# One weight ring of five buffers, and PSUM banks of its own for the first block's second half, in a diffusion layer with PEER experts

## The chip, the cores and the metric

The kernel runs on one core of a Trainium2 chip. The metric is the device time of one execution in microseconds (us). A core has a matrix engine (PE, TensorE), VectorE (DVE), ScalarE (ACT), GpSimd (POOL) and SyncE (SP). Each takes its instructions in order. Matmuls write into PSUM, which has eight banks of 512 float32 in each of 128 partitions; the other data lie in SBUF. Transfers are issued by SP, ACT and POOL and run on 16 DMA engines.

## What is computed

One layer over 1024 latent tokens of width 1024, with 256 context tokens that give keys and values alone. All is float32. Cut to what matters:

```python
hx = modulate(rmsnorm(xs, norm1_g), sh1, sc1)
q, k, v, u, ga, gc = split(hx @ w_in)                  # w_in: 1024 x 5632
y_att  = attend(rope(norm(q)), rope(norm(k)) + k_ctx, v + v_ctx) @ w_attn_o
a, b   = split(u); g = a * sigmoid(b)
g      = depthwise_conv(g, width 31)                   # over the tokens, per channel
y_conv = silu(layernorm(g + conv_b)) @ w_conv_o
xs = xs + g1 * ((sigmoid(ga) * y_att + sigmoid(gc) * y_conv) @ w_out)
h  = modulate(rmsnorm(xs, norm2_g), sh2, sc2)
# PEER: 8 heads, two halves of 128 keys, the 16 best of each, the 16 best of their sums
s = h @ peer_wq, scored against peer_keys; eid, w = the 128 experts of a token and their weights
act = gelu(peer_u[eid] . h)                            # 128 rows of 1024 for each token
xs  = xs + g2 * sum((w * act) * peer_v[eid])
out = rmsnorm(xs, final_norm_g)
```

## The kernel before

**Blocks.** The tokens go in four blocks of 256 (two tiles of 128). For each block `phase1` makes four streams. `convolution` projects w_in's columns for the convolution into pb and pa and runs 31 taps for each of eight channel groups on DVE (`tap`, into z and odd). `attention` projects q (pq of 128 columns), norms and turns it, and does eight heads for each tile (pS the scores, pr the softmax, pt its transposes, po the product). `rest` is the second half of a block: the two gated products (`gated`, pg and py), between them the norm over channels (`channel_norm`, pmu and pvar, for which all taps must be done), the product with w_out (po of 256 columns, into dT), `second_norm` (transposes pt of dT, of xn and of h2T), and eight times `scores` (pq of 256 columns, then s2). `choosing` picks the 16 best on DVE. When two heads of a tile are chosen, their experts can be gathered.

**The experts.** `dots` gathers one row of peer_u for each of 128 tokens by an indirect DMA of POOL (tile u, 512 KB), and one DVE operation multiplies and sums it: one dot for each of 128 experts of a tile, 1024 in all. Three buffers hold u (`U_ROWS`) while the blocks run; when they are over, four more come from the space of the blocks (`U_MORE`). For five tiles (`GATHERED`) `sums_by_choice` gathers peer_v likewise (tile vv; three buffers, later nine) and PE adds it up in y by matmuls of 32 columns. For the other three (`DENSE`, tiles 1, 2 and 4) the dense stage at the end (`dense`) builds matrices of weights in four quarters (DVE makes B and A, PE pc, ACT C), and multiplies them with the whole of peer_v, loaded as vd: acc, 32 loads for each quarter. `finish_token_tile` does the last norm and the store.

**What sets the order.** Instructions are not issued as the streams write them. Each is recorded with a cost (`Paced`), and `Pace` keeps a model of each engine's time and emits next what can start first; nearly equal starts go by the rank of the stream. On DVE while the blocks run that rank is `RANK = "vumbahc"`: v rows, then dots (u), then a block's second half (m), the builds (b), attention (a), choosing (h), and the convolution with its taps (c) last. The names of a tile that is overwritten enter the model (`evicts`), so the number of buffers of a pool changes the order on all engines. All of it is at line 262 in the profile; groups are told apart by their tiles.

**Buffers that matter here.** `wload` loads a weight tile of 512 KB into the ring w; it has four buffers (`WEIGHTS`), and the transposed tokens hT of the start use the same ring. `bank` gives one of two PSUM banks (pool psm) to all that the blocks compute except pS: convolution, attention, and second half alike. `pair` halves one of them. The pool psy has one buffer of two banks: at the start pk (keys and values, one bank) takes it, later y. `rsqrt` has two scratch tiles of its own in the pool att for the norm over channels.

Of the kernel before, what the change touches and what calls it, by code (L numbers as in the profile page):

```python
# [8 lines left out]
F32 = mybir.dt.float32  # L9
# [3 lines left out]
AF = mybir.ActivationFunctionType  # L13
# [26 lines left out]
KEPT = 4  # L40
WEIGHTS, SLOTS, U_ROWS, V_ROWS, U_MORE, V_MORE = 4, 4, 3, 3, 4, 6

# [251 lines left out]
def layer_kernel(ctx: ExitStack, tc: tile.TileContext, a, out):  # L294
# [12 lines left out]
    exq = pool(ctx, "exq", 2)  # L307
    psy = pool(ctx, "psy", 1, space=PSUM)
    ps = pool(ctx, "ps", 1, space=PSUM)
# [18 lines left out]
    def pair(name):  # L328

        t = bank(name)  # L330
        return t[:, 0:256], t[:, 256:512]
# [4 lines left out]
    def rsqrt(y, v, n):  # L336

        home, tag = (small, n) if n < P else (att, "")
        t = home.tile([P, n], F32, name="rs_t", tag=f"rs_t{tag}", bufs=1)
        b = home.tile([P, n], F32, name="rs_b", tag=f"rs_b{tag}", bufs=1)  # L340
        V.tensor_scalar(t.bitcast(I32), v.bitcast(I32), 1, None, op0=OP.logical_shift_right)
        V.tensor_scalar(y.bitcast(I32), t.bitcast(I32), -1.0, float(0x5F3759DF), op0=OP.mult, op1=OP.add)
        for _ in range(3):
            V.tensor_tensor(out=b, in0=y, in1=y, op=OP.mult)
            V.scalar_tensor_tensor(out=b, in0=b, scalar=-0.5, in1=v, op0=OP.mult, op1=OP.mult)
            V.scalar_tensor_tensor(out=y, in0=b, scalar=1.5, in1=y, op0=OP.add, op1=OP.mult)
# [266 lines left out]
    def phase1(b, t0, Tb):  # L613
# [6 lines left out]
        mine = blocks[b] = {}  # L620

        def convolution():
            while b and "gated" not in blocks[b - 1]:
# [111 lines left out]
        def gated(g0, wo, src, first, mg):  # L735

            for j in range(KC):
                yield "PE"
                wg, w2 = wload(a["w_in"], g0 + j * P), wload(a[wo], j * P)
                pg, py = pair("pg")  # L740
                mm8(pg[:, :Tb], wg, lambda kc: mine["hT"][:, kc, :Tb])
                mm8(py[:, :Tb], w2, lambda kc: src[:, kc, :])
                tb = att.tile([P, Tb], F32, name="tg", tag="gt")
                S.activation(tb, pg[:, :Tb], AF.Tanh, scale=0.5)
                if first:
                    V.scalar_tensor_tensor(out=mg[:, j, :], in0=tb, scalar=1.0, in1=py[:, :Tb], op0=OP.add, op1=OP.mult)
                else:
                    V.scalar_tensor_tensor(out=tb, in0=tb, scalar=1.0, in1=py[:, :Tb], op0=OP.add, op1=OP.mult)
                    V.scalar_tensor_tensor(out=mg[:, j, :], in0=tb, scalar=0.5, in1=mg[:, j, :], op0=OP.mult, op1=OP.add)

        def channel_norm(z):

            yield "PE"
            pmu = bank("pmu")
            for j in range(KC):
# [4 lines left out]
            for j0 in range(0, KC, 4):  # L760
                yield "DVE"
                sq = [att.tile([P, Tb], F32, name="zsq", tag="zsq", bufs=4) for _ in range(4)]
                for j in range(4):
                    V.tensor_tensor(out=z[:, j0 + j, :], in0=z[:, j0 + j, :], in1=mu, op=OP.subtract)
                    S.activation(sq[j], z[:, j0 + j, :], AF.Square)
                pvar = bank("pvar")
                for j in range(4):
# [19 lines left out]
        def second_norm(i, dT, h2T):  # L787
# [5 lines left out]
            for half in range(2):  # L793
                pt = bank("pt")
                for q in range(4):
# [9 lines left out]
            for half in range(2):  # L805
                pt = bank("pt")
                for q in range(4):
# [6 lines left out]
            for half in range(2):  # L814
                pt = bank("pt")
                for q in range(4):
                    PE.transpose(pt[:, q * P:(q + 1) * P], h2T[:, half * 4 + q, ts], ident)
                S.activation(xn[:, half * 512:(half + 1) * 512], pt, AF.Copy)
            S.dma_start(h2_d[row, :], xn)

        def scores(q, h2T):
# [3 lines left out]
            q2 = att.tile([P, 2, Tb], F32, name="q2", bufs=1)  # L825
            pqs = pair("pq")
            for b in range(2):
# [4 lines left out]
            for i in range(nt):  # L832
                yield "PE"
                s2 = bank("s2")
                for b in range(2):
# [5 lines left out]
        def rest():  # L841
# [10 lines left out]
            for j in range(KC):  # L852
                yield "PE"
                w = wload(a["w_out"], j * P)
                po = bank("po")
                mm8(po[:, :Tb], w, lambda kc: mg[:, kc, :])
# [180 lines left out]
    def finish_token_tile(ti, y):  # L1037
# [5 lines left out]
        Q.dma_start(fin, a["final_norm_g"].to_broadcast([P, D]))  # L1043
        V.tensor_tensor(out=y, in0=y, in1=ga2, op=OP.mult)
        V.tensor_tensor(out=fo, in0=fo, in1=y, op=OP.add)
        ss = small.tile([P, 1], F32, name="ss", tag="ss1")
        S.activation(y, fo, AF.Square, accum_out=ss)
        r_ = rstd_of(ss, 1, D)
        V.scalar_tensor_tensor(out=fo, in0=fo, scalar=r_, in1=fin, op0=OP.mult, op1=OP.mult)
        S.dma_start(out[row, :], fo)  # L1050

    def dense():
# [67 lines left out]
        def products():  # L1120
# [4 lines left out]
            for n, ti in enumerate(DENSE):  # L1125
                finish_token_tile(ti, ysum[:, n, :])

        return building(), products()

    def sums_by_choice(ti, eiT, cT):  # L1130

        y = psy.tile([P, D], F32, name="y")
        for r in range(32):
# [9 lines left out]
            while j0 < 4:  # L1143
# [9 lines left out]
                for half in range(2):  # L1153
                    hs = slice(half * 512, (half + 1) * 512)
                    for j, vv in group[-1:] + group[:-1]:
                        PE.matmul(y[32 * j:32 * j + 32, hs], lhsT=Z[:, j, 32 * rr:32 * rr + 32], rhs=vv[:, hs],
                                  start=(r == 0), stop=(r == 31))
# [111 lines left out]
```

## Time and profile before

| | |
|---|---|
| median of 3 runs | 4075.68 us (4071.9 to 4087.45) |
| profiled execution: time | 4076.87 us |
| profiled execution: span of the instructions | 4075.1 us |
| PE busy | 3193.5 us (78%) |
| DVE busy | 2637.7 us (65%) |
| POOL busy | 1859.3 us (46%) |
| ACT busy | 759.9 us (19%) |
| moved by DMA | 1189.76 MB, mean 292 GB/s |

Busy time of PE is that of its matmul records, which overlap a little; a float32 matmul stands in the trace as two records, a transpose and a bf16 matmul as one. "PEclk" is the share of the 2.4 GHz that the chip grants the matrix engine, 1.00 or 0.50 at any moment. "DMA share" is the mean busy share of the 16 DMA engines. A row "A <- B: us, times" in the waits says how long A's engine stood idle until B released it.

### The profile page before, as it was taken

What the parts mean: (1) busy time and instruction counts of PE and PEld (TensorE: products, weight loads), DVE (VectorE), ACT (ScalarE), POOL (GpSimd) and SP (SyncE); (2) the same over time, 40 slices, a digit from 0 to 9 for tenths busy, and PEclk for the clock granted to TensorE, in tenths of its full rate; (3) what the DMA queues carried; (4) which work ended last, traced back from release to release, by engine and by line L of the source; (5) the groups of instructions that cost most, each with busy time, mean ns of one, the idle gap of its engine ahead of it and who ended that gap; (6) DMA issues with size and microseconds to landing.
All of it is one profiled execution on the core that took longest, in us unless ns stands there. A gap on an engine that the chain in (4) does not pass through costs nothing. (4 is left out here: it accounts for less than half of the span.)

```text
span 4075.1 us, 49507 instructions
## 1 busy us (share of the span) xinstructions
PE 3193.5 (78%) x17804; PEld 2009.4 (49%) x17804; DVE 2637.7 (65%) x7114; ACT 759.9 (19%) x1439; POOL 1859.3 (46%) x1672
## 2 busy tenths in 40 slices
PE   5898997779878889978656875468978866885994
PEld 2576885568655558745445742133443324332331
DVE  2493158887768896778888569685784458356102
ACT  3335113331012331023321020120020002001000
POOL 0000000443545553445444445686787768676550
PEclk9999998889889899989877987569979887997997
DMA  8530553779999889998779998899999999999993
GB/s 291 162 101 7 150 151 104 239 232 314 317 320 310 296 303 331 347 333 297 255 230 284 316 347 278 297 345 389 385 362 398 406 379 362 402 406 370 352 374 136
DMA packets 649558, 1189.76 MB, mean 292 GB/s; under 512 B 36825, under 2 KB 387393, under 8 KB 649312
## 3 DMA queue, kind: packets, MB, share of 16 engines
q0 software_dynamic: 239616, 872.52, 58.8%
q1 hardware_dynamic: 394736, 294.88, 23.6%
q10 hardware_dynamic: 14960, 19.19, 1.3%
q8 instruction: 140, 2.29, 0.2%
q14 instruction: 106, 0.87, 0.1%
HBM read 1168.62 MB, written 17.83 MB: 291 GB/s over the span
## 5 line engine op out<-in xcount | busy, mean ns | idle before, releaser
L262 POOL DMA_INDIRECT u<-in_peer_u,ei x1024 | 1117.2, 1091 | 1735.5 <-DVE tx L262 721.6
L262 DVE CUSTOM_DVE_ANT_0 u<-u,h 128x1024 f32<-128x1024 f32 x1024 | 1244.5, 1223 | 671.9 <-DMA u<-in_peer_u,ei 662.2
L262 POOL DMA_INDIRECT vv<-in_peer_v,eiT x640 | 739.1, 1155 | 392.1 <-PE y L262 192.5
L262 PE MATMUL y<-vv,Z 128*32 128x512 f32 x2560 | 509.2, 722 | 247.1 <-DMA vv<-in_peer_v,eiT 246.9
L262 PE MATMUL acc<-vd,C 128*128 128x512 f32 x1536 | 697.9, 607 | 0.0
L262 PEld LDWEIGHTS acc<-vd,C 128*128 128x128 f32 x1536 | 288.8, 194 | 398.3 <-issue 394.7
L262 PEld LDWEIGHTS y<-vv,Z 128*32 128x32 f32 x2560 | 95.2, 122 | 523.0 <-issue 280.0
L262 PE MATMUL pc<-A,B 128*128 128x32 bf16 x4608 | 179.1, 192 | 149.6 <-DVE A L262 131.5
L262 PEld LDWEIGHTS <-B 128*128 128x128 bf16 x4608 | 167.3, 118 | 215.2 <-DVE A L262 116.3
L262 PE MATMUL pq<-h2T,w 128*128 128x256 f32 x1024 | 248.0, 397 | 14.2 <-ACT q L262 7.3
L262 PE MATMUL pg<-hTb,w 128*128 128x256 f32 x1024 | 238.1, 385 | 6.7 <-DVE tg L262 3.6
L262 PEld LDWEIGHTS pq<-h2T,w 128*128 128x128 f32 x1024 | 198.4, 198 | 74.7 <-issue 23.9
L262 DVE SCALAR_TENSOR_TENSOR z<-g,dw,z 128x256 f32<-128x256 f32 x480 | 230.4, 480 | 0.0
L262 PE MATMUL pS<-kT,qT 128*128 128x512 f32 (+1 forms) x384 | 179.6, 585 | 54.8 <-ACT pr L262 54.8
L262 PE MATMUL pb<-hTb,w 128*128 128x256 f32 (+2 forms) x896 | 211.3, 389 | 13.0 <-DMA w<-in_w_in 9.2
L262 ACT ACTIVATE C<-pc 128x512 f32<-128x512 f32 x96 | 104.6, 1096 | 622.3 <-PE pc L262 373.9
L262 PEld LDWEIGHTS pg<-hTb,w 128*128 128x128 f32 x1024 | 195.8, 193 | 40.5 <-DVE tg L262 5.5
L262 DVE SCALAR_TENSOR_TENSOR odd<-g,dw,odd 128x256 f32<-128x256 f32 x448 | 215.1, 480 | 0.0
L262 PEld LDWEIGHTS pb<-hTb,w 128*128 128x128 f32 x896 | 171.8, 196 | 46.0 <-issue 19.6
L262 PEld LDWEIGHTS po<-pT,vS 128*128 128x128 f32 x1280 | 165.4, 204 | 37.0 <-issue 17.3
L262 PE MATMUL po<-pT,vS 128*128 128x128 f32 x1280 | 173.5, 290 | 6.6 <-ACT pT L262 6.0
L262 DVE TENSOR_TENSOR B<-io__15984,i12T 128x2048 bf16<-128x2048 bf16 x96 | 117.4, 1223 | 63.2 <-PE pc L262 57.3
(209 smaller groups left out, 3547.7 us busy)
## 6 DMA issues: line engine op xcount, KB each, us to landing
w<-in_w_in SPq DMA_DIRECT2D x160, 512.0 KB, 6.3
vd<-in_peer_v SPq DMA_DIRECT2D x128, 512.0 KB, 8.1
w<-in_peer_wq SPq DMA_DIRECT2D x64, 512.0 KB, 7.5
wm<-in_w_mod SPq DMA_DIRECT2D x48, 512.0 KB, 6.4
w<-in_w_attn_o SPq DMA_DIRECT2D x32, 512.0 KB, 6.1
w<-in_w_conv_o SPq DMA_DIRECT2D x32, 512.0 KB, 5.4
w<-in_w_out SPq DMA_DIRECT2D x32, 512.0 KB, 9.9
u<-in_peer_u,ei POOLq DMA_INDIRECT x1024, 7.0
```

Source lines behind the costliest of these rows:

```text
L262: go = lambda: f(*args, **kw)
```

## The change

Four things, all in how buffers are given out; the work is the same but for the last norm.

1. `WEIGHTS` is 5 instead of 4. The space comes in part from `rsqrt`, whose two scratch tiles of 256 columns are now taken from the ring zsq (four buffers, otherwise for the squares of the norm over channels).
2. The pool psy has two buffers of one bank instead of one of two banks. So pk of the start has two banks in turn, and y is two tiles of 512 columns, each a half.
3. In block 0 `gated`, `channel_norm`, `second_norm`, `scores` and the product with w_out take their PSUM tiles from psy (`bank2`), not from the pair that convolution and attention use. In the other blocks they stay where they were.
4. `finish_token_tile` works on the two halves one after the other, with two partial sums of squares and one addition more.

```diff
-WEIGHTS, SLOTS, U_ROWS, V_ROWS, U_MORE, V_MORE = 4, 4, 3, 3, 4, 6
+WEIGHTS, SLOTS, U_ROWS, V_ROWS, U_MORE, V_MORE = 5, 4, 3, 3, 4, 6
...
-    psy = pool(ctx, "psy", 1, space=PSUM)
+    psy = pool(ctx, "psy", 2, space=PSUM)
...
     def pair(name):
 
-        t = bank(name)
+        return halved(bank(name))
+
+    def halved(t):
         return t[:, 0:256], t[:, 256:512]
...
-        home, tag = (small, n) if n < P else (att, "")
-        t = home.tile([P, n], F32, name="rs_t", tag=f"rs_t{tag}", bufs=1)
-        b = home.tile([P, n], F32, name="rs_b", tag=f"rs_b{tag}", bufs=1)
+        t, b = ((small.tile([P, n], F32, name=m, tag=f"{m}{n}", bufs=1) if n < P else
+                 att.tile([P, n], F32, name=m, tag="zsq", bufs=4)) for m in ("rs_t", "rs_b"))
...
+        def bank2(name):
+
+            return bank(name) if b else psy.tile([P, 512], F32, name=name, tag="y")
...
-                pg, py = pair("pg")
+                pg, py = halved(bank2("pg"))
...
-            pmu = bank("pmu")
+            pmu = bank2("pmu")
...
-                pt = bank("pt")
+                pt = bank2("pt")
...
-            pqs = pair("pq")
+            pqs = halved(bank2("pq"))
...
-                po = bank("po")
+                po = bank2("po")
...
-        V.tensor_tensor(out=y, in0=y, in1=ga2, op=OP.mult)
-        V.tensor_tensor(out=fo, in0=fo, in1=y, op=OP.add)
-        ss = small.tile([P, 1], F32, name="ss", tag="ss1")
-        S.activation(y, fo, AF.Square, accum_out=ss)
-        r_ = rstd_of(ss, 1, D)
+        ss = small.tile([P, 2], F32, name="ss", tag="ss2")
+        for h in range(2):
+            hs = slice(h * 512, (h + 1) * 512)
+            V.tensor_tensor(out=y[h], in0=y[h], in1=ga2[:, hs], op=OP.mult)
+            V.tensor_tensor(out=fo[:, hs], in0=fo[:, hs], in1=y[h], op=OP.add)
+            S.activation(y[h], fo[:, hs], AF.Square, accum_out=ss[:, h:h + 1])
+        V.tensor_tensor(out=ss[:, 0:1], in0=ss[:, 0:1], in1=ss[:, 1:2], op=OP.add)
+        r_ = rstd_of(ss[:, 0:1], 1, D)
...
-        y = psy.tile([P, D], F32, name="y")
+        y = [psy.tile([P, 512], F32, name="y") for _ in range(2)]
```

The order changes on every engine, as the model behind it sees other buffers. Two places follow. A row is an instruction, its tiles, the size of its output, and how many of it stand in a row.

First place, PE, block 0's second norm (transposes pt of dT, xn and h2T), before. The matmuls pb and pq<-w,hTb are block 1's projections for convolution and attention.

```order
L262 MATMUL pt<-ident,dT 128x128 x4
L262 MATMUL pb<-hTb,w 128x256 x10
L262 MATMUL pt<-ident,dT 128x128 x4
L262 MATMUL pt<-ident,xn 128x128 x8
L262 MATMUL pt<-ident,h2T 128x128 x8
L262 MATMUL pt<-ident,dT 128x128 x8
L262 MATMUL pt<-ident,xn 128x128 x8
L262 MATMUL pt<-ident,h2T 128x128 x8
```

The same place now.

```order
L262 MATMUL pt<-ident,dT 128x128 x8
L262 MATMUL pb<-hTb,w 128x256 x15
L262 MATMUL pt<-ident,xn 128x128 x8
L262 MATMUL pq<-w,hTb 128x128 x8
L262 MATMUL pb<-hTb,w 128x256 x3
L262 MATMUL pt<-ident,h2T 128x128 x8
L262 MATMUL pq<-w,hTb 128x128 x3
L262 MATMUL pt<-ident,dT 128x128 x8
L262 MATMUL pq<-w,hTb 128x128 x5
L262 MATMUL pb<-hTb,w 128x256 x14
L262 MATMUL pq<-w,hTb 128x128 x8
L262 MATMUL pb<-hTb,w 128x256 x2
```

Block 1's projections stand between the steps of the second norm now, where before only one group of them did; the second token tile's xn transposes follow these rows.

Second place, PE, the end of block 1's gated products and the close of block 0's choice (pt of eid and e, whose results the v gathers and the dense stage use; pt of act is the end of the first tile's dots), before.

```order
L262 MATMUL pg<-z,w 128x256 x8
L262 MATMUL pt<-ident,eid 128x128
L262 MATMUL pt<-ident,e_1320 128x128 x2
L262 MATMUL pb<-hTb,w 128x256 x38
L262 MATMUL pq<-w,hTb 128x128 x8
L262 MATMUL pb<-hTb,w 128x256 x2
L262 MATMUL pq<-w,hTb 128x128 x4
L262 MATMUL pt<-ident,act 128x128
```

The same transposes of eid, e and act now.

```order
L262 MATMUL po<-pT,vS 128x128 x10
L262 MATMUL pt<-ident,eid 128x128
L262 MATMUL pt<-ident,e_1320 128x128 x2
L262 MATMUL pmu<-z,ones_d 128x256 x8
L262 MATMUL pt<-ident,act 128x128
L262 MATMUL pg<-hTb,w 128x256 x2
L262 MATMUL pvar<-zsq,ones_d 128x256
```

Before, block 1's norm over channels and all 256 of its gated matmuls (pg) stood ahead of the close of block 0's choice. Now that close and the end of the first tile's dots come first, and the gated matmuls behind them.

## Rows read from the trace of the kernel before

**Rows 1.** The page: span; DMA busy in tenths, 40 equal slices.

```profile
span 4075.1 us, 49507 instructions
DMA  8530553779999889998779998899999999999993
```

**Rows 2.** Tile u, 720 to 973 us: count, duration, first and last start.

```profile
L262 DVE CUSTOM_DVE_ANT_0 u<-u,h x96: 1203/1224/1279, 720.3 to 966.7; 128x1024 f32<-128x1024 f32 x96
```

**Rows 3.** Busy time by stage; columns as the first line says.

```profile
core 0: us, PE busy (x) PEld busy (x) DVE busy (x) ACT busy (x) POOL busy (x), PEclk, DMA share, GB/s
720.00:1074.00 354.00, 286.94 (x1380) 234.35 (x1379) 281.46 (x826) 93.94 (x179) 136.83 (x132) 0.91 0.86 274
1074.00:2614.00 1540.00, 1169.71 (x5379) 809.00 (x5380) 1206.79 (x3631) 324.09 (x640) 747.54 (x682) 0.88 0.91 302
2614.00:2749.00 135.00, 79.56 (x1355) 49.33 (x1355) 112.56 (x218) 27.29 (x29) 109.40 (x85) 0.65 0.95 340
2749.00:3032.00 283.00, 245.58 (x1741) 119.92 (x1738) 203.25 (x367) 30.46 (x37) 210.21 (x170) 0.90 1.00 383
3032.00:3425.00 393.00, 291.02 (x2022) 128.83 (x2020) 223.96 (x409) 28.66 (x34) 290.30 (x254) 0.84 1.00 385
3425.00:3793.00 368.00, 290.63 (x2030) 128.22 (x2027) 205.39 (x374) 29.20 (x35) 257.36 (x235) 0.87 1.00 384
3793.00:4018.00 225.00, 224.71 (x861) 82.90 (x858) 5.00 (x12) 2.43 (x7) 102.48 (x110) 1.00 0.89 334
4018.00:4075.10 57.10, 0.23 (x1) 0.00 (x0) 21.62 (x61) 4.60 (x8) 0.00 (x0) 0.55 0.27 92
```

**Rows 4.** DVE's waits from 1074 to 2614 us: total, times, longest.

```profile
DVE u L262 <- DMA u<-in_peer_u,ei: 262.7, 200, 19.2
```

**Rows 5.** Windows of tile u alone: DVE (dots), POOL (gathers), clock, DMA.

```profile
1074.00:2614.00 1540.00, 606.96 (x498) 541.58 (x501) 0.88 0.91 302
2749.00:3793.00 1044.00, 430.60 (x356) 396.30 (x354) 0.87 1.00 384
```

**Rows 6.** Windows of tile vv alone: PE, weight loads, POOL (gathers), clock, DMA.

```profile
2749.00:3793.00 1044.00, 184.39 (x1200) 36.62 (x1200) 361.57 (x303) 0.87 1.00 384
3793.00:4018.00 225.00, 55.79 (x464) 12.18 (x464) 102.48 (x110) 1.00 0.89 334
```

**Rows 7.** PE in order of time: start, duration, instruction, idle before and releaser.

```profile
583.62 2.32 PE L262 MATMUL po<-mg,w 128*128 128x256 f32 x10
...
625.84 1.97 PE L262 MATMUL pt<-ident,xn 128*128 128x128 f32 x8 [9.66 <-ACT xn L262]
...
640.94 1.97 PE L262 MATMUL pt<-ident,xn 128*128 128x128 f32 x8 [8.07 <-ACT xn L262]
...
661.80 3.82 PE L262 MATMUL pS<-kT,qT 128*128 128x512 f32 x6
...
674.30 2.36 PE L262 MATMUL pS<-kT,qT 128*128 128x512 f32 x6
...
679.92 3.72 PE L262 MATMUL pq<-h2T,w 128*128 128x256 f32 x16 [0.69 <-ACT pT L262]
```

**Rows 8.** The page's groups: records, busy us, mean ns, idle before, releaser.

```profile
L262 PE MATMUL pg<-hTb,w 128*128 128x256 f32 x1024 | 238.1, 385 | 6.7 <-DVE tg L262 3.6
...
L262 PE MATMUL pb<-hTb,w 128*128 128x256 f32 (+2 forms) x896 | 211.3, 389 | 13.0 <-DMA w<-in_w_in 9.2
```

**Rows 9.** Tile pmu, 880 to 930 us: count, duration, first and last start.

```profile
L262 PE MATMUL pmu<-z,ones_d x16: 379/379/795, 898.7 to 902.9; 128*128 128x256 f32 x16
```

**Rows 10.** Waits from 2100 to 2200 us: total, times, longest.

```profile
PE pmu L262 <- DVE z L262: 48.5, 1, 48.5
```

**Rows 11.** Windows around that wait; columns as in rows 3.

```profile
2126.00:2170.00 44.00, 0.81 (x2) 0.72 (x3) 38.49 (x128) 1.06 (x1) 21.75 (x19) 0.50 0.73 225
2170.00:2184.00 14.00, 9.02 (x22) 6.75 (x22) 13.05 (x40) 1.63 (x4) 5.62 (x6) 0.63 0.72 225
2184.00:2300.00 116.00, 111.44 (x512) 96.06 (x510) 77.19 (x187) 18.27 (x42) 42.41 (x42) 1.00 1.07 335
```

More of the change, by code (lines that the diff above doesn't have):

```diff
@@ L765, in channel_norm @@
                     S.activation(sq[j], z[:, j0 + j, :], AF.Square)
-                pvar = bank("pvar")
+                pvar = bank2("pvar")
                 for j in range(4):
@@ L805, in second_norm @@
             for half in range(2):
-                pt = bank("pt")
+                pt = bank2("pt")
                 for q in range(4):
@@ L814, in second_norm @@
             for half in range(2):
-                pt = bank("pt")
+                pt = bank2("pt")
                 for q in range(4):
@@ L833, in scores @@
                 yield "PE"
-                s2 = bank("s2")
+                s2 = bank2("s2")
                 for b in range(2):
@@ L1125, in products @@
             for n, ti in enumerate(DENSE):
-                finish_token_tile(ti, ysum[:, n, :])
+                finish_token_tile(ti, [ysum[:, n, h * 512:(h + 1) * 512] for h in range(2)])
         return building(), products()
     def sums_by_choice(ti, eiT, cT):
-        y = psy.tile([P, D], F32, name="y")
+        y = [psy.tile([P, 512], F32, name="y") for _ in range(2)]
         for r in range(32):
@@ L1154, in sums_by_choice @@
                     hs = slice(half * 512, (half + 1) * 512)
+                    yh = y[half]
                     for j, vv in group[-1:] + group[:-1]:
-                        PE.matmul(y[32 * j:32 * j + 32, hs], lhsT=Z[:, j, 32 * rr:32 * rr + 32], rhs=vv[:, hs],
+                        PE.matmul(yh[32 * j:32 * j + 32, :], lhsT=Z[:, j, 32 * rr:32 * rr + 32], rhs=vv[:, hs],
                                   start=(r == 0), stop=(r == 31))
```

## The prediction

> **What bounds the kernel now.** I read the span and its slices, then the windows by stage [rows 1 to 3]. The run has three regimes. Until 720 us no dot runs, since the experts of the first tokens aren't chosen yet, and the DMA engines have slices of zero, three and five tenths [rows 1, 2]. From 720 to 2614 us the four blocks run beside the u gathers, which have three buffers. From 1074 us on no engine there is full (VectorE 1207 of 1540 us, PE 1170, DMA 0.91), but the rest hangs on VectorE: 263 of its 333 us of idle time are waits for a u row to land [rows 3, 4], and 498 dots take the 1540 us, 3.09 us each [rows 5]. From 2614 to 3793 us, in the dense stage, with seven buffers for u and nine for v, the DMA share is 0.95 and then 1.00 in three stretches one after the other [rows 3]: the transfers are the bound. The dense product's last quarter, 3793 to 4018 us, is PE's, with 224.7 us busy of 225; 57 us of final norms follow. So the price of a gather depends on where it runs. In the three full stretches 356 u, 303 v and 96 vd (32 for each quarter) take 1044 us, 1.38 us each [rows 5, 6]; in the blocks a dot comes, with all that lies around it, at 3.09 us.
>
> **Term 1, the first dot.** The first block's second half and the next block's projections share two PSUM banks. The trace shows the cost at the second norm: from the last w_out matmul (583.62 + 2.32 = 585.9 us) to the first score projection (679.92) lie 94 us, and PE stands still for 9.66 and 8.07 us of them ahead of the transposes of xn [rows 7]. In the new order 15 and 29 projection matmuls stand in those two places, and three heads of block 1's attention, whose scores take 3.82 us at the first and 2.36 at the last [rows 7], stand behind the first score projections instead of ahead of them. 48 pb matmuls instead of 80 stand in the stretch: 32 at 211.3/448 = 0.47 us (a program matmul is two records) [rows 8], 15 us. With 8.5 us for the heads and 6 us for their transposes and waits the stretch loses 17.7 + 8.5 + 15 + 6 = 47 us. From there to the first dot, by the order at the rows' durations, PE has 13 us more to do and VectorE 12. The first dot moves from 720.3 [rows 2] to about 687 us, 33 earlier; bounds 20 and 45.
>
> **Term 2, to dot 129.** Dots outrank the convolution's taps. As they begin earlier, 72 tap operations of block 1 that stood ahead of the first dot now stand among the dots, and 249 of the 256 gated matmuls of block 1 move from ahead of dot 129 to behind it (order, second place). Block 1's second half begins at 898.7 us now [rows 9]; it will wait for the last tap, which stands two dots ahead of dot 129, until about 1005. Between dot 1 and dot 129 VectorE has 7 us less to do than the 281 us of its row, in a stretch of 354 [rows 3], and fewer weights travel beside it. Between 300 us (VectorE nearly full) and 347 (354 less 7) I take the middle, 326, since both rows that bound it are as near: dot 129 at 1013 instead of 1074, 61 us earlier.
>
> **Term 3, to the first build of the dense stage.** The moved second half lies here now. In the order 670 dots stand ahead of the first B, where 626 stood, and 26 v rows more are gathered in this stretch. 44 dots at 606.96/498 = 1.22 us [rows 5] are 54 us of VectorE; 36 us of other operations come along with the moved blocks; each dot waits 263/498 = 0.53 us for its row [rows 4], 23 us. So 1540 + 113 = 1653. By the cadence it is 542 x 3.09 = 1675. Below: if the added work runs in time that is idle now, 1600. Above: if the DMA share stays at 0.91, 71 more gathers and some 38 more weight tiles at the full stretches' 1.38 us add 150 us to 0.91 x 1540 = 1401 us of DMA work, and 1551/0.91 = 1705. I take 1662, near the sum of VectorE, which has the waits: the dense stage begins at 2675 instead of 2614, 61 us later.
>
> **Term 4, the dense stage.** By the counts in the order: up to the first acc 12 transfers fewer and 13 us less of VectorE, so 135 us become 122. In the three full stretches 707 transfers instead of 755, 48 x 1.38 = 66 us less, so 1044 become 978; PE, with 245.6 + 291.0 + 290.6 = 827 us busy [rows 3], stays under that. In the last quarter PE has 12 v rows fewer, 48 records at 55.79/464 = 0.12 us [rows 6], 6 us: 219. Together 85 us less. If PE or the vd loads set the pace, only 60 come back; at the most 100.
>
> **What I cost at nothing.** The fifth weight buffer: PE's longest wait for a weight tile, in sum, is the 9.2 us at pb [rows 8], in stretches that VectorE sets; zero, bounds -10 and 0. The reciprocal root's scratch in the ring of the squares: its users follow one another anyway. The second bank for the key projections: the order up to there differs by a few rows. The norm in halves: VectorE and ScalarE take turns on halves, where one waited for a whole; of eight such norms four lie open in the last 57 us; zero, bounds -2 and 2. If ScalarE's turn is late, VectorE's next operation, the sum of the two halves, waits for it, and the store behind.
>
> **Sum.** 1013 + 1662 = 2675; + 122 + 978 + 219 + 57 = 4051 us of span; with the 1.8 us between span and time 4053, against 4076.9 for the profiled execution. That one is 1 us over the median of the runs, so 4052 on the median's scale, -0.6%.
>
> **A rule against it.** Block 3 shows what block 1 will meet. There PE waited 48.5 us for z [rows 10], and in that stretch the granted clock was 0.50, the 1.2 GHz level; 2170 to 2184 us stands at 0.63 and the stretch behind at 1.00, 2.4 GHz [rows 11]. The Trainium skill (TensorE: Matmul & The Clock Gate, What's actually happening) says that throttled is the default state of this clock and that activity lifts it; the row agrees. By that rule the wait for the taps is paid twice, as idle time and again in slow matmuls behind it, by this row some 5 us, and the sum would be 4057.
>
> **The rivals.** (a) *A wash.* What the dense stage loses and what the blocks gain are the same gathers, moved. If the blocks take 1686 us instead of 1662, the dense stage begins at 2699, and the end is 4076. For it: 3.09 us for a dot and the waits belong to three u buffers, which stay. Against: the first dot is earlier, into idle DMA time.
> (b) *The starved second half, slower.* Block 1's second half begins 106 us later than now, with 249 x 238.1/512 = 116 us of matmuls [rows 8] moved behind dot 129, and each block's chain (projections, norm, scores, choice) hands the delay on to the next. With dot 129 at 1034 us and the 1705 behind it, the dense stage begins at 2739, and the end is 4116, +1.0%. Past a beginning of 2719 us it is over 0.5% slower. For it: PE idles about 100 us ahead of that half, and the DMA share leaves little room. Against: VectorE's work is the same in sum.
> (c) *The blocks close up.* If part of VectorE's 333 us of idle time goes and the stretch takes 1610 us, the end is 4000.
> (d) *The banks do nothing.* If the two waits at the second norm come from its own chain, the first dot gains the reordering alone, 20 us, and the end is about 4066. It counts with (a).
>
> **How the numbers follow.** This kernel's measurement can tell about 0.5%, 20 us, from no change. A gain of over that, with (c): 0.43, of which (c) 0.12. A wash, with (d): 0.33. Slower, mostly (b): 0.24. The range leaves out about a tenth on each side: it ends at 4000, which is (c), and at 4115, which is (b). The likeliest case's own range is 4020 to 4055.
>
> **What would show it.** The first dot between 675 and 700 us. No wait of over 5 us ahead of the transposes of xn. PE waiting about 100 us for z ahead of block 1's pmu, until about 1005 us, at the clock's lower level. About 670 dots ahead of the first pc, and that at about 2675 us. Then 1.38 us for each transfer, and a last quarter of about 219 us. I am wrong if the first pc comes later than 2719 us, if the blocks' dots come at over 3.2 us, or if the dense stage is less than 60 us shorter.

## The result and the profile after

The changed kernel takes 4147.3 us (median of four runs) where the kernel before takes 4081.5 on the same chip: a ratio put at 1.017, interval 1.0142 to 1.0198 (the two medians by themselves divide to 1.016). It is slower; 4052 was forecast, in a range up to 4115.

The page of the changed kernel answers [rows 1]: the span, and the DMA engines' busy tenths in 40 slices.

```profile
span 4145.2 us, 49524 instructions
DMA  8530455767999998997877899889999999999993
```

Its windows by stage answer [rows 3] (columns in the first line). The cuts are the same events: first dot, dot 129, first build of the dense stage (here and below its first product pc on TensorE; the first B on VectorE stands some 3 us ahead of it), first dense product, end of the first quarter, last quarter, final norms.

```profile
core 0: us, PE busy (x) PEld busy (x) DVE busy (x) ACT busy (x) POOL busy (x), PEclk, DMA share, GB/s
705.00:1028.00 323.00, 160.13 (x805) 124.28 (x804) 274.51 (x808) 84.40 (x148) 141.64 (x130) 0.74 0.75 235
1028.00:2784.50 1756.50, 1333.42 (x6103) 939.30 (x6102) 1297.29 (x3818) 345.79 (x691) 824.96 (x751) 0.88 0.90 298
2784.50:2905.00 120.50, 76.47 (x1314) 47.45 (x1314) 103.55 (x194) 25.36 (x25) 96.73 (x74) 0.68 0.92 324
2905.00:3192.00 287.00, 254.94 (x1806) 122.49 (x1804) 197.53 (x363) 32.48 (x41) 220.36 (x178) 0.91 1.01 392
3192.00:3869.00 677.00, 561.00 (x3988) 253.03 (x3986) 392.86 (x722) 57.49 (x72) 499.29 (x432) 0.90 1.01 390
3869.00:4088.00 219.00, 218.60 (x816) 81.92 (x813) 5.12 (x12) 2.20 (x6) 93.05 (x99) 1.00 0.85 318
4088.00:4145.20 57.20, 0.22 (x1) 0.00 (x0) 23.00 (x72) 5.67 (x16) 0.00 (x0) 0.52 0.26 92
```

The whole loss is in the second row. The dense stage begins at 2784.5 us instead of 2614, 170.5 later, and gives back 100 (1360.7 us instead of 1461.1). In the stretch itself VectorE's busy time rises by 90 us (1206.8 to 1297.3), TensorE's by 164 (1169.7 to 1333.4), the stretch by 216.5. The row above is the other half of it: TensorE is busy for 160 of 323 us there, at a granted clock of 0.74, where it was busy for 287 of 354.

What TensorE did instead shows in its order of time ahead of block 1's second half (start, duration, instruction; in brackets the idle time before it and what ended that):

```profile
939.42 0.47 PE L262 MATMUL pt<-ident,eid 128*128 128x128 f32 x1 [38.78 <-DVE eid L262]
955.15 0.69 PE L262 MATMUL pt<-ident,e 128*128 128x128 f32 x2 [15.25 <-DVE e L262]
955.62 5.24 PE L262 MATMUL pmu<-z,ones_d 128*128 128x256 f32 x12
977.63 1.22 PE L262 MATMUL pmu<-z,ones_d 128*128 128x256 f32 x2 [16.76 <-DVE z L262]
1013.30 1.22 PE L262 MATMUL pmu<-z,ones_d 128*128 128x256 f32 x2 [34.45 <-DVE z L262]
```

In [rows 9] all 16 of these pmu records start between 898.7 and 902.9 us. Now the last of them starts at 1013.9, and TensorE has waited four times, 105 us in all, for VectorE: 54 us for the close of block 0's choice (eid, e) and 51 for the last taps of block 1 (z), both behind dots. The granted clock falls and comes back with it:

```profile
955.00:1013.00 58.00, 6.94 (x16) 4.69 (x16) 52.14 (x108) 0.00 (x0) 25.97 (x27) 0.53 0.75 234
1028.00:1100.00 72.00, 68.74 (x315) 59.09 (x314) 46.87 (x95) 12.05 (x28) 26.25 (x27) 1.00 1.01 320
```

[rows 11] showed the same at block 3: there 0.50 of the full clock (1.2 GHz) while TensorE stands, here 0.53, and 1.00 (2.4 GHz) in the next busy stretch in both.

Several waits grew in the rest of the blocks. VectorE's longest two, from 1028 to 2784.5 us, answering [rows 4] (total, times, longest):

```profile
DVE u L262 <- DMA u<-in_peer_u,ei: 336.0, 266, 18.2
DVE g L262 <- ACT tb L262: 52.5, 9, 27.6
```

The second of them was, from 1074 to 2614 us before:

```profile
DVE g L262 <- ACT tb L262: 23.8, 7, 10.3
```

And TensorE's from the first dot to the first build, after:

```profile
PE y L262 <- DMA vv<-in_peer_v,eiT: 204.2, 47, 12.2
PE pt L262 <- DVE eid L262: 55.8, 5, 38.8
PE pt L262 <- ACT s2s L262: 52.4, 6, 22.0
PE pmu L262 <- DVE z L262: 51.2, 2, 34.4
PE pt L262 <- DVE act L262: 40.0, 4, 33.0
```

and before:

```profile
PE y L262 <- DMA vv<-in_peer_v,eiT: 137.3, 34, 10.6
PE pmu L262 <- DVE z L262: 53.0, 2, 48.5
...
PE pt L262 <- ACT s2s L262: 29.2, 7, 13.4
...
PE pt L262 <- DVE eid L262: 16.6, 2, 9.4
```

The 206 v rows (183 before) that are gathered ahead of the dense stage are waited for with 67 us more. The wait for z is no longer than it was in sum (51 against 53 us): it lay almost whole at block 3 [rows 10] and lies at block 1 now. What grew are the waits for the choice (s2s, eid: 24 and 39 us more) and for the end of a tile's dots (act, from 2 to 40 us).

### The profile page after: what moved, and what is told of

Its sections match the earlier page's. It is cut to its first block, busy times and chain, and to the rows that moved or that the text cites. A ratio compares the mean times of both kernels' runs of the same rounds, so it can differ in the third digit from the quotient of the medians.

```text
span 4145.2 us, 49524 instructions
## 1 busy us (share of the span) xinstructions
PE 3199.5 (77%) x17804; PEld 2017.9 (49%) x17804; DVE 2642.2 (64%) x7138; ACT 764.8 (18%) x1457; POOL 1881.2 (45%) x1672
## 4 chain that ended last, share of the span: by engine, by line
PE 29%; DMA 29%; DVE 16%; issue 16%; POOL 9%; ACT 1%; POOLq 0%; ACTq 0%; SPq 0%; DVEq 0%
DMA u<-in_peer_u,ei 15%; DMA vv<-in_peer_v,eiT 10%; PE acc L262 7%; POOL u L262 6%; DVE u L262 6%; PE y L262 5%; PE pg L262 4%; PE pq L262 3%; POOL vv L262 3%; PE po L262 2%; PE pb L262 2%; PE pk L262 1%; PE pc L262 1%; DVE z L262 1%; DVE odd L262 1%
## 5 line engine op out<-in xcount | busy, mean ns | idle before, releaser
L262 POOL DMA_INDIRECT u<-in_peer_u,ei x1024 | 1130.2, 1104 | 1709.5 <-DVE tx L262 712.0
L262 POOL DMA_INDIRECT vv<-in_peer_v,eiT x640 | 748.0, 1169 | 452.5 <-PE y L262 265.0
L262 PE MATMUL y<-vv,Z 128*32 128x512 f32 x2560 | 524.2, 722 | 294.5 <-DMA vv<-in_peer_v,eiT 292.6
L262 PE MATMUL pS<-kT,qT 128*128 128x512 f32 (+1 forms) x384 | 170.0, 561 | 42.5 <-ACT pr L262 42.2
L262 PEld LDWEIGHTS po<-pT,vS 128*128 128x128 f32 x1280 | 177.2, 217 | 36.0 <-issue 16.6
L262 PE MATMUL po<-pT,vS 128*128 128x128 f32 x1280 | 185.6, 304 | 7.1 <-ACT pT L262 6.4
L262 PE MATMUL pt<-ident,pr 128*128 128x128 f32 x640 | 103.2, 293 | 88.9 <-ACT s2s L262 52.4
```

Source lines behind the costliest of these rows:

```text
L262: go = lambda: f(*args, **kw)
```

## The experiments

Names that the expectations use. **S**: block 1's second half waits behind dots, and the delay is handed on. **V**: the blocks hang on VectorE's work. **D**: each dot ahead of the dense stage costs. **R**: the new rings themselves cost, whatever the order. **O**: the order that the planner makes of them costs. **C**: the loss belongs to one chip. All runs in one table, from their traces: the first dot, the start of the last pmu of block 1 (us), TensorE's idle time from the one to the other, the first build of the dense stage ("blocks end"), dots + v rows ahead of it, the length of the dense stage, and the ratio to the kernel before on the same chip with its interval. Each set ran on one chip; sets without a trace of the kernel before are read against set 2's. The length of the dense stage differs between sets by up to 8% (last section), so it is compared among sets 1 to 3, or between the first two rows and set 4. Of the diffs only the lines that matter are shown.

| run | dot 1 | pmu | idle | blocks end | ahead | dense | ratio |
|---|---|---|---|---|---|---|---|
| before | 720 | 903 | 47 | 2614 | 626+183 | 1461 | |
| after | 705 | 1014 | 157 | 2785 | 670+206 | 1360 | 1.017 |
| *set 1* shared_pair | 740 | 919 | 43 | 2673 | 640+180 | 1544 | 1.004 (1.0021 to 1.006) |
| four_weights | 683 | 968 | 133 | 2693 | 662+198 | 1497 | 0.9979 (0.9958 to 1.0001) |
| hold_taps | 719 | 1057 | 186 | 2807 | 695+212 | 1460 | 1.0168 (1.0113 to 1.0222) |
| taps_first | 769 | 923 | 42 | 2684 | 571+169 | 1640 | 1.03 (1.0256 to 1.0344) |
| *set 2* before_again | 723 | 905 | 46 | 2615 | 626+182 | 1581 | |
| changed | 707 | 1013 | 156 | 2779 | 670+206 | 1493 | 1.0183 (1.0139 to 1.0227) |
| hold_taps_small | 722 | 982 | 121 | 2727 | 663+198 | 1507 | 1.0094 (1.0072 to 1.0115) |
| thin_dots | 727 | 891 | 33 | 2507 | 626+181 | 1612 | 0.981 (0.9792 to 0.9828) |
| *set 3* cap_40 | 707 | 898 | 45 | 2669 | 579+186 | 1637 | 1.0195 (1.0142 to 1.0249) |
| cap_four | 678 | 879 | 55 | 2640 | 579+186 | 1629 | 1.0146 (1.0086 to 1.0205) |
| rank_a | 754 | 910 | 42 | 2682 | 573+174 | 1630 | 1.0224 (1.0173 to 1.0275) |
| near | 721 | 907 | 50 | 2672 | 642+179 | 1564 | 1.0043 (1.0016 to 1.007) |
| *set 4* old_order | 716 | 900 | 49 | 2648 | 638+186 | 1443 | 1.0012 (0.999 to 1.0035) |
| plan_five | 704 | 1002 | 154 | 2790 | 675+207 | 1378 | 1.0227 (1.019 to 1.0265) |

**One part of the change at a time.** The first run gives block 0's second half its shared pair of banks back; the second takes the fifth weight buffer away.

```diff
-            return bank(name) if b else psy.tile([P, 512], F32, name=name, tag="y")
+            return bank(name)
```

> The changed kernel with one part undone: block 0's second half takes its PSUM tiles from the shared pair again; the ring of five, the halves of y and the halved norm stay. In its order all of block 1's gated matmuls stand ahead of dot 129 again, and 638 dots stand ahead of the first pc (626 before the change, 670 with it). Theory S (block 1's second half is starved, because dots begin earlier and outrank its taps): about 4080 us, dense stage from about 2625 us, block 1's pmu at about 900 us. Theory R (the ring, the y halves or the halved norm cost the time): about 4147 us, as with the change. Theory D (no place matters, each dot that stands ahead of the dense stage costs: 44 dots, 66 us): 12 dots more than before, about 4100 us.

```diff
-WEIGHTS, SLOTS, U_ROWS, V_ROWS, U_MORE, V_MORE = 5, 4, 3, 3, 4, 6
+WEIGHTS, SLOTS, U_ROWS, V_ROWS, U_MORE, V_MORE = 4, 4, 3, 3, 4, 6
```

> The changed kernel with four weight buffers instead of five, all else as changed. In its order block 1's pmu still stands among the first tile's last dots (112 dots ahead of it; 72 before the change, 126 with it), and 662 dots stand ahead of the first pc. S: still slow, 4130 to 4150 us, with PE waiting some 100 us ahead of block 1's second half. R, if the ring is what costs: about 4080 us. D: 36 dots more than before the change, about 4135 us.

Neither half makes the loss: 1.004 and 0.998. Both together make 1.017, so the parts don't add. S came out nearly for the first run (2673 us for the blocks' end, where it had 2625) and missed the second, where it had a ratio of over 1.01; R has the second and misses the first. With the banks and without the fifth buffer block 1's second half is some 63 us late and the idle time 133 us, the blocks end 78 us late, and the dense stage gives all of it back (84 us); a late half is not yet a slower kernel.

**A late second half without the change.** Two edits of the kernel before hold block 1's last taps back until dots have been recorded (90 dots and three channel groups; 30 dots and one group; `begun` counts the dots).

```diff
             for k0 in range(0, TAPS, 4):
+                while b == 1 and j >= 5 and begun[0] < 90:
+                    yield None
```

> The kernel before the change, with one thing added to its order: the taps of block 1's last three channel groups are recorded only after 90 dots. No buffer and no bank changes. Its order then has block 1's pmu behind dot 129, as the change does, and 695 dots ahead of the first pc. S: the change's loss without the change, 4130 to 4160 us, blocks longer by about 200 us and dense stage shorter by about 120. R: as before, about 4080 us. D: 69 dots more, about 4185 us.

> The kernel before with a small dose of the late second half: only the taps of block 1's last channel group wait, for 30 dots. 104 dots stand ahead of block 1's pmu (72 before, 126 with the change), 663 ahead of the first pc; first dot 13 us of VectorE work earlier. S: between before and change, +20 to +45 us, with 40 to 60 us of PE's idle time ahead of block 1's pmu. Theory V (the blocks hang on VectorE, each dot ahead of the dense stage costs there what the dense stage gives back): within 15 us of the kernel before. With four_weights, whose dose was alike and whose time was that of before, a time within 15 us would say that a small dose is won back.

Late by 152 and 77 us, the kernel before loses 1.7% and 0.9%, with its old rings and banks: as S said, less than D for the first, and more than V for the second. The wait is of the kind that the change has, TensorE standing behind VectorE's dots (first of the two, from 950 to 1070 us):

```profile
PE pt L262 <- DVE act L262: 85.3, 1, 85.3
```

So an order with a late second half, without the new rings, reproduces the loss in size. It doesn't yet say that the change has no other. Nor is lateness alone a measure of the loss: 77 us late with 663 dots ahead cost 0.9% here, 63 us late with 662 dots ahead cost nothing in `four_weights`.

**Taps ahead of dots, in the change.**

```diff
-RANK, RANK_PE, RANK_LATE = "vumbahc", "muvbahc", "vubmahc"
+RANK, RANK_PE, RANK_LATE = "vcumbah", "muvbahc", "vubmahc"
```

> The changed kernel with the convolution's taps ahead of the dots in the rank of the model, in all blocks; all buffers and banks as changed. In its order block 1's pmu has 58 dots ahead of it (126 with the change alone) and 571 dots stand ahead of the first pc. S: the loss goes, 4060 to 4090 us: block 1's second half from about 890 us, dense stage from about 2520 us and about 1500 us long. R: about 4147 us. D: 55 dots fewer than before the change, about 4000 us.

The wait goes (idle 42 us) and the kernel is slower still, 1.03; S, which had 4060 to 4090 us, misses. The first dot comes 46 us later than in the kernel before, and 571 dots lie ahead instead of 670, so the dense stage is longer. D falls with it: the fewest dots ahead, and blocks that end at 2684, 69 us after before's.

**The change again, the kernel before again, and VectorE's work cut.** The third is the kernel before in its own order, with each dot taken over 256 of its 1024 columns (it leaves out the rest of the sum; the dots have a line of their own, L1013).

> The changed kernel as it is, beside the others on one chip. Theory S (block 1's second half begins late, PE stands idle there for about 105 us, and what follows in the blocks hangs on PE's order, so the delay stays): 1.015 to 1.02 times the kernel before, first pc about 170 us later, dense stage about 100 us shorter. Theory C (the loss is of the one chip on which the first runs were made, by its DMA rate): within 0.5% of the kernel before here.

> The kernel before the change, for a profile on the same chip as the others. S and C: the time of the kernel before on this chip; block 1's pmu 180 us after the first dot, first pc about 1900 us after it.

> The kernel before, instruction for instruction in the same order on all engines, but each dot multiplies and sums 256 of the 1024 columns, so a dot takes VectorE about 0.42 us instead of 1.22 (its result is another); gathers and all else are unchanged. V: between dot 129 and the first pc 498 dots give back 0.8 us each, 400 us at the most, and the blocks shorten by over 200 us. S: the blocks' end hangs on PE's order, of which the dots are no part, and on the gathers: they shorten by less than 100 us.

C falls: 1.0183 on another chip. The thin dots decide on V. The stretch from dot 129 to the first build, with thin dots:

```profile
1049.00:2507.00 1458.00, 1156.92 (x5380) 804.11 (x5381) 823.00 (x3634) 324.73 (x642) 663.03 (x681) 0.89 0.95 320
```

and in the kernel before on that chip:

```profile
1073.00:2615.00 1542.00, 1168.30 (x5380) 808.19 (x5381) 1207.40 (x3632) 323.72 (x639) 729.66 (x681) 0.88 0.91 302
```

384 us less work on VectorE shorten the stretch by 84 (the blocks end 108 us earlier in all). The dots then wait longer for their rows:

```profile
DVE u L1013 <- DMA u<-in_peer_u,ei: 427.0, 308, 8.1
```

against 234 us on that chip before. The engine with the longest wait list was not by itself what the blocks hang on: of each microsecond taken from it a fifth came off the stretch. With a DMA share of 0.95 the transfers may be what holds the thin dots' stretch; no run tests that.

**Taking the wait out of the change.** The first token tile's dots stop at 40 until block 1's last tap is issued (with five weight buffers, then with four); another rank; and a control, the kernel before with one constant of its planner changed.

```diff
+            while ti == 0 and k >= 40 and not tapped:
+                yield None
```

> The change, with the dots of the first token tile held at 40 until the last tap of block 1's second half of channels is emitted; all else is the change's. S (the loss is block 1's second half, which waits for taps that dots go ahead of): the mean over that half starts at 890 to 930 us instead of 1013, TensorE's idle time from the first dot to it falls from 157 to under 70 us, and the blocks close by 2620 to 2680 instead of 2779; but only about 580 dots instead of 670 lie ahead of the dense stage, which then takes about 1600 to 1650 instead of 1493, so the time stays within 1% of the change's (ratio to before 1.00 to 1.025). V (the blocks hang on VectorE's work): its work ahead of the dense stage falls by some 128 us, the blocks close by as much earlier wherever block 1's half starts. R (the ring itself is dear): the blocks still close 100 us or more later than before's, whatever the idle time.

> The kernel above (first tile's dots held at 40 until block 1's last tap) with four weight buffers instead of five. S: block 1's second half at 890 to 930, blocks closed by 2590 to 2650, about 580 dots ahead, dense stage 1580 to 1640: ratio 0.99 to 1.02. R: 40 us or more earlier at the dense stage than the same kernel with five buffers, since the ring is what makes the blocks long; S: within 30 us of it.

```diff
-RANK, RANK_PE, RANK_LATE = "vumbahc", "muvbahc", "vubmahc"
+RANK, RANK_PE, RANK_LATE = "vmcubah", "muvbahc", "vubmahc"
```

> The change with the planner's order of VectorE's streams turned: a block's second half first, its taps next, dots behind both (before and the change: second half, dots, taps). About 573 dots ahead of the dense stage. S: neither the taps nor the second half waits behind dots: the second halves start as in the run that put the taps ahead of all (923, 1534, 2209 us) and take no longer than before's (585, 604, 344 from the mean over channels to the scores), so the blocks close by 2560 to 2620; dense stage about 1620 to 1660; ratio 1.00 to 1.02. If the second halves are as long as with the taps ahead of all (598, 672, 390), the blocks close at 2680 and the ratio is about 1.03: then what made them long there is not the taps' rank over them but fewer products and dots fitting into TensorE's and VectorE's pauses.

```diff
-NEAR = 0.1
+NEAR = 0.11
```

> The kernel before with one constant of the planner (how close two pieces of work count as equally due) at 0.11 instead of 0.10: no buffer, bank or operation differs, only the order, by a little: 642 dots ahead of the dense stage instead of 626, block 2's second half behind 12 more dots, block 3's behind 26 more. It measures how much an order without meaning moves the time. S: block 1's second half as before (905), blocks 2 and 3 some 10 to 40 us later, dense stage some 30 us shorter: ratio 0.995 to 1.01. If the ratio is 1.015 or more, the loss of the change says little on its parts, since any order moves it by as much.

With the cap, block 1 is on time and the blocks end 110 us earlier than the change's, as S said. The kernel is no faster for it (1.0195). The blocks still end 54 us later than before's (set 2), with 43 fewer transfers ahead, and the dense stage is 57 us longer. A wait of the same kind has opened at the close of block 2's choice (2100 to 2220 us, then the window of the wait itself):

```profile
PE pt L262 <- DVE e L262: 82.6, 1, 82.6
```

```profile
2117.00:2200.00 83.00, 0.42 (x4) 0.23 (x4) 72.79 (x247) 2.88 (x4) 35.62 (x35) 0.52 0.75 224
```

VectorE is busy there for 73 of 83 us with other work while TensorE stands. The run with four buffers is 29 us earlier at the dense stage, at the edge between what R and S expected; it is as much earlier at its first dot (678 and 707), so nothing of it arises in the blocks that follow. The rank puts the second halves where S wanted them (910, 1515, 2159 us) and misses the blocks' end by 60 us or more (2682 against 2560 to 2620). (Before's rank isn't as its expectation has it: in `RANK` dots stand ahead of the second half.) The expectation's other branch had 2680 for long second halves, and the last two are long: 638 and 418 us from the last pmu to the end of the scores, where before's are 602 and 338. What makes them long isn't shown; it isn't that taps go ahead of them. The control moves the blocks' end by 57 us with nothing changed but the order, though the time only by 0.4%: a shift of that size at the blocks' end needs no cause but another order, and the 1.004 of `shared_pair` is no more than the control's. The loss of the change is four times that.

**The rings or the order?** That is open after these. The planner places each step by its own reckoning of when a buffer comes free, so a larger ring changes the order as well as the chip's waits. Two kernels take these apart. In the first the chip has all that the change brings, but the planner reckons with the rings of before; in the second the chip has four weight buffers and the planner reckons with five; the banks and the halved norm stay as changed in both.

```diff
+    wpool.old["w"], psy.old["y"], psm.old["mm"] = ("w", 4), ("y", 1), ("mm", 2)
+    att.old.update(rs_t=("rs_t", 1), rs_b=("rs_b", 1), zsq=("zsq", 4))
```

> The change whole, five weight buffers, the banks of its own and the halved norm, but the planner reckons with the rings of before (four weights, one shared pair of banks, a scratch of its own), so that the order is before's up to block 2's second half and close to it behind that (block 1's second half behind 72 dots, block 2's behind 264 against before's 262, block 3's behind 497 against 484; 638 dots ahead of the dense stage against 626). O (the loss comes by the order that the planner makes of the new rings): block 1's second half at 890 to 915 us, the blocks close by 2600 to 2680 (the run with the changed constant: 2672 with 642 dots), dense stage 1540 to 1580, ratio 0.985 to 1.006. R (the buffers themselves make the run longer, by what they let start early on the queues and banks): the blocks close by 2720 or later, ratio 1.01 or more, though the order is before's.

```diff
+        n = 5 if tag == "w" else bufs or self.bufs
```

> The change with four weight buffers in the chip, while the planner reckons with five: nearly the change's order (block 1's second half behind 120 dots against the change's 126, block 2's behind 318 against 322, block 3's behind 539 against 536; 675 dots ahead of the dense stage against 670) without its ring. O: block 1's second half at 990 to 1030, blocks closed by 2740 to 2810, dense stage 1480 to 1500, ratio 1.01 to 1.025, like the change. R (the ring itself): like the run with four weight buffers and their own order: 968, 2693, ratio 0.995 to 1.003.

The rings with nearly the order of before (638 dots ahead, 626 before) cost nothing that can be measured: 1.0012. Block 1's pmu, in that run (line 262 has moved to 267 there, and to 264 in the other):

```profile
L267 PE MATMUL pmu<-z,ones_d x16: 379/540/795, 894.4 to 899.5; 128*128 128x256 f32 x16
```

The order without the fifth buffer costs all of it: 1.0227, and the blocks end at 2790 us, where the change's end at 2785. (The dense stages came out some 100 us shorter than expected in both runs, as in the first two rows of the table; see the last section.) TensorE's waits from 935 to 1030 us are the change's:

```profile
PE pt L264 <- DVE eid L264: 47.7, 1, 47.7
PE pmu L264 <- DVE z L264: 36.9, 2, 34.9
PE pt L264 <- DVE e L264: 15.8, 1, 15.8
```

R falls and O stands. The fifth buffer itself makes a difference of 5 us at the blocks' end, between two orders that are nearly the same (675 and 670 dots ahead).

## Why the prediction was wrong

**Term 1 was half right.** The second norm lost its waits as forecast: the xn transposes have no idle time ahead of them now, where [rows 7] had 9.66 and 8.07 us (start, duration, instruction).

```profile
591.30 17.53 PE L262 MATMUL po<-mg,w 128*128 128x256 f32 x80 [1.50 <-DMA w<-in_w_out]
...
616.89 1.04 PE L262 MATMUL pt<-ident,xn 128*128 128x128 f32 x8
...
634.70 1.04 PE L262 MATMUL pt<-ident,xn 128*128 128x128 f32 x8
...
648.29 1.97 PE L262 MATMUL pq<-h2T,w 128*128 128x256 f32 x8 [1.34 <-DMA w<-in_peer_wq]
```

From the end of w_out (608.8 us) to the first score projection are 39.5 us, forecast 47, before 94. But w_out itself ends 23 us later than in [rows 7], and the term began its count behind it. The same 2538 matmul records of TensorE stand up to there in both kernels; TensorE is idle for 16 us more, 15 of them for block 0's normed q (qraw). From 100 to 394 us, before and then after:

```profile
PE pt L262 <- DVE qraw L262: 3.8, 2, 2.4
PE pt L262 <- DVE qraw L262: 18.7, 2, 12.6
```

The first dot moved by 15 us, to 705 [rows 2], where I had 33. The missing 18 go with the order that the planner makes for five weight buffers: with four for chip and planner (`four_weights`) the wait for qraw is 3.6 us and the first dot comes at 683, where the term had 687; with four in the chip and five for the planner (`plan_five`) they are 11.0 us and 704. The prediction had costed the fifth buffer at zero.

**Term 2 was right in its number.** 323 us from dot 1 to dot 129, forecast 326; dot 129 is at 1028, forecast 1013, and 18 us of that are term 1's. The pmu's wait until "about 1005" ended at 1013. But the 100 us that it put on z were 51 us for z and 54 for the close of block 0's choice.

**Term 3 is the step that failed.** It said 1662 us; the stretch from dot 129 to the first build took 1756.5. Its count of VectorE's work was right to the microsecond: 54 + 36 us more, measured 90.5; 670 dots ahead, as counted. Two things were wrong. It let each added dot wait 0.53 us for its row, 23 us in all, but VectorE's idle time grew by 126 us (333 to 459), 73 of them waits for u [rows 4]. And it took VectorE, "which has the waits", for what sets the end, so that the TensorE work which term 2 had moved out of its stretch never came back in the sum: 127 us less there, 164 us more here. Rival (b) named 116 us of it and put it aside because VectorE's work is the same in sum. The thin dots show, in the order of before, that VectorE's sum doesn't set the end. What does, TensorE's moved work, the transfers or the chain through all three, no run shows. The Trainium skill (Perfetto Trace Analysis, Identifying the Most-Contended Engine) goes by occupancy for VectorE, ScalarE and GpSimd and by HBM utilization for the transfers, and has the engine with the highest optimized first. VectorE's 1207 of 1540 us are 78%; the transfers' 302 GB/s [rows 3] are, by estimate, 84% of the 358 GB/s that the page's section Roofline has as a core's share. So by that rule too VectorE wasn't the engine to price the stretch by, and the thin dots agree. The cadence of the dots came out at 1756.5/542 = 3.24 us, past the 3.2 at which I had said that I would be wrong; the windows of tile u in the stretch and in the three full stretches behind it, as in [rows 5] (VectorE, GpSimd):

```profile
1028.00:2784.50 1756.50, 660.42 (x542) 583.13 (x546) 0.88 0.90 298
2905.00:3869.00 964.00, 383.04 (x317) 358.90 (x312) 0.91 1.01 390
```

**Term 4 was right.** 120.5 + 964 + 219 + 57.2 us, forecast 122 + 978 + 219 + 57: 1361 against 1376. With 317 u, 297 v (the row below, as in [rows 6]) and 96 vd the three stretches take 964/710 = 1.36 us for a transfer; I had counted 707 at 1.38.

```profile
2905.00:3869.00 964.00, 172.93 (x1168) 34.77 (x1168) 360.75 (x297) 0.91 1.01 390
```

So the gain was there, 100 us, and the blocks spent more than it: their end, with 67 more transfers ahead, came 171 us later.

**What was costed at nothing.** On the chip it was nothing: with the order of before all of it together is 1.0012. Their price lies in the order that the planner makes with them, in terms 1 to 3, and there it was mis-sized. The norm in halves lies in the last stretch at 57.2 us against 57.1.

**The rule against it.** The Trainium skill (TensorE: Matmul & The Clock Gate, What's actually happening) takes throttled for this clock's default, lifted by activity; the trace agrees, with 0.53 while TensorE stood and 1.00 behind it. It is at most a small part of the loss: from dot 129 to the first build the granted clock is 0.88 before and after. No run separates the 5 us that the prediction read off for it.

**The rivals.** (b), the starved second half, is nearest to what happened, at a chance of 0.24, and too small: 2739 against 2785. It took term 1 and 2 nearly as they came (dot 129 at 1034) and 1705 us behind it: 1551 us of DMA work at a share of 0.91. The share came out at 0.90, so that the transfers were busy for 0.90 x 1756.5 = 1581 us. Its bound was thus nearer than term 3's sum, but that doesn't make the transfers the cause: the thin dots moved as many bytes as the kernel before (320 GB/s x 1458 us and 302 x 1542 us, some 466 MB) in 84 us less. No run takes transfers out of the blocks, so this stays untested. (a) and (c) are out. (d) had 20 us for the first dot, near the 15 measured, but that is luck: the waits for xn, which it took for the norm's own, are gone.

**What stays open.** The loss is made by the order, and an order with a late second half, in the old rings, makes a loss of that size. By the table 111 of the 171 us are there when block 1's last pmu starts (1014 against 903), and 60 more come from there to the blocks' end (1771 us against 1711). Every run with whole dots but the kernel before itself has 1725 to 1788 us in that second stretch, the control 1765: so the 60 are no more than other orders cost, and no run wins a late pmu back before the dense stage. That compares orders which differ in more than this. And none of the four runs in which the half is on time (`taps_first`, `cap_40`, `cap_four`, `rank_a`) is a faster kernel, 1.0146 to 1.03, since others of its waits opened or the dense stage grew: an order with the late half is shown to be enough for such a loss, not that the late half is the whole of the change's. That two parts lose together what neither loses alone is explained as the planner's order, not shown step by step.

## What to carry to other kernels

An engine that waits a lot for its inputs is not thereby what a stage hangs on: before a stretch is priced by one engine's work, list every engine's busy time and the transfers' share in it, and carry work that one term moves out of a stretch into the term where it lands. Where a planner sets the order, a resource's price has two parts, what it does on the chip and what the planner does with it; give the chip the resource and keep the old order, and the other way round, and the two are apart in two runs. A control with an order changed for no reason gives a first measure of how much of a difference is only that; one control is one sample.

## What the runs showed of the hardware

The dense stage took 1461 and 1443 us in two sets of runs and 1581 and 1564 in two others, with about as many transfers left to do (kernels before and near or old_order), while the blocks ended at the same time: 2614 and 2615 us in the two runs of the kernel before. In the second of these the transfers are slower though the stage is theirs (us, busy times, clock, DMA share, GB/s):

```profile
2750.00:3911.00 1161.00, 882.88 (x6073) 403.57 (x6066) 650.26 (x1182) 92.01 (x111) 765.40 (x671) 0.84 0.94 352
```

[rows 3] has 383 to 385 GB/s at a share of 1.00 in its three full stretches. So a stage bound by transfers differed by 8% between sets, and the blocks' end by 1 us: only ratios within a set compare here. It isn't the number of the chip that tells the sets apart: sets 3 and 4 carry the same one on record, and the kernel before has medians of 4212 and 4076 us in them. The Trainium skill (Perfetto Trace Analysis, Roofline) gives 358 GB/s as a core's share of the memory where both cores of a pair use it, and more where one is alone; 384 and 352 lie on either side, but no run here shows what another core did. The change's own ratio was nearly the same in both kinds of set, 1.017 and 1.0183, since its dense stage gained 100 us in the one and 88 in the other.
